# Hybrid conformer / RWKV-7 block: the A products of the RWKV chunks on 64 rows, and two scratch pools in PSUM resized

## The chip, the cores and the metric

The kernel runs on one core of a Trainium2 chip. The metric is the device time of one execution in microseconds (us), lower is better. The engines named below are TensorE (PE, with its weight loads shown apart as PEld), VectorE (DVE), ScalarE (ACT), GpSimd (POOL) and SyncE (SP), which issues the transfers.

## The reference, cut to what matters

One decoder block on x of 2048 tokens by 1024 channels, in fp32. A normalized and modulated input goes through one wide projection; its columns feed a convolution branch, an RWKV-7 branch and gates; both branches are projected, merged, projected once more and added to x. The part that the change touches is in the RWKV branch, a recurrence with a 64 x 64 state for each of 16 heads:

```python
def step(state, inp):
    r_t, w_t, k_t, v_t, kk_t, b_t = inp
    sk = jnp.einsum('bhvk,bhk->bhv', state, kk_t)
    state = (state * w_t[:, :, None, :] - sk[..., None] * b_t[:, :, None, :]
             + v_t[..., None] * k_t[:, :, None, :])
    return state, jnp.einsum('bhvk,bhk->bhv', state, r_t)
```

The kernel computes this recurrence in chunks of 64 tokens. Within a chunk every token's r and kk vector must meet every earlier token's k and b vector of the same head. These dot products over the head's 64 channels are what is called the A products here; a head's channels never meet another head's.

## The kernel before, in words

**Blocks, groups, pairs.** The sequence is cut into four blocks of 512 tokens (NB, TB), a block into eight chunks of 64 (NCH, CH). A tile of 128 partitions holds the channels of two heads, 64 rows each, which the code calls a pair; two pairs make a group, so a block has four groups (the loop from line 874, which calls `group`, line 575, which steps two `pair` generators, line 457, in the order ORD). The large projections go through `mm3k` (lines 198 to 206): each fp32 product is made of three products of fp32r halves, and its matmuls, all of line 205, fill TensorE's queue between everything else.

**One pair.** `pair` builds two tensors of 128 partitions, KR and BK, which hold, for each two chunks, 256 columns: those of the even chunk and those of the odd chunk, 128 each (kk and r side by side in KR, b and k in BK). KR is written on lines 498 and 523, BK on lines 512 and 518. Then come the A products (lines 528 to 541): for each half of the block (c4, four chunks) and each head (hh) four fp32 matmuls of 128 x 128 with BK's columns as weights and KR's columns streamed, into one PSUM bank pA; line 539 masks the bank on DVE and writes it to Asb. A tile's two heads lie in different row halves and a matmul contracts over all 128 rows. So line 531 first copies each head's 64 rows of BK, on ACT, into BKz, a tile whose other 64 rows were set to zero once (lines 287 to 289), and line 537 contracts BKz with all rows of KR. BKz has one buffer: the second half's copies wait for the first half's matmuls. The trace shows each of these fp32 matmuls as two records, so 512 of them are 1024 records. Later POOL scales BK in place (line 564) and PE transposes it (line 570).

**What follows.** `group` inverts the small triangular blocks (POOL, lines 625 to 630, and matmuls 659 and 668), and then runs the chain over the eight chunks (lines 677 to 702): matmuls 686, 691 and 697, each followed by a DVE instruction (688, 693, 701) that reads the chain's PSUM tile `xo`; line 701 writes the state S, which line 686 of the next chunk reads. Lines 599 and 710 are further products on 64-wide tiles: line 599 takes 64 rows of its operands and writes 64 partitions and goes from one half to the other with every matmul; line 710 contracts over all 128 rows and alternates the written half; line 691 stays in one half for all four matmuls of a chunk.

**PSUM.** Eight banks: two for the projections (pool pm, tag "main"), one for late products (pl), one for the convolution's accumulator (pc), PXB = 2 for the chain's `xo` (px) and PAB = 2 for scratch (pa, tag "aux"). Scratch serves, in this order within a pair, pw, pq, pss, pA four times, pv, pb and pt twice, and in a group pv of line 595. At the very start `hprep0` (line 379) fills four banks with the first projections (T_LORA and T_K in pm, T_R and T_V in px), and `shifted` (line 424) reads them later.

**What sets the order.** The program runs under a tile framework that finds the dependences, inserts the waits and writes the order of each engine's queue from a simulated timeline of its own; only the ORD and FILL tables and a few priorities are by hand. Every engine then works through its queue in that order.

Of the kernel before, what the change touches and what calls it, by code (L numbers as in the profile page):

```python
# [9 lines left out]
F32 = mybir.dt.float32  # L10
# [3 lines left out]
ALU = mybir.AluOpType  # L14
# [4 lines left out]
P = 128  # L19
D = 1024  # L20
KT = D // P
TB = 512
NTT = TB // P
CH = 64
NCH = TB // CH
# [10 lines left out]
HB = 8  # L36
HXB = 7
GG = 0
PXB, PAB = 2, 2
VVT, SHT, RKT, RHT, YT = "r", "sh", "k", "sh", "M"  # L40
ORD = (0, 0, 1, 0, 1, 1)
OE, LE, CE = 0, 0, 1
# [40 lines left out]
def hybrid_block(ctx: ExitStack, tc: tile.TileContext, x, vecs, convk, w2a2, final_g, ada, w_in, w_co, w_ro, w_o, crow, out,  # L83
                 seq=2048, groups=(0, 1, 2, 3), phase2=True, dbg=None):
    nc = tc.nc
# [36 lines left out]
    def rsqrt(y, x_, pool, eng, t=None):  # L122
        if t is None:
            t = pool.tile(list(x_.shape), F32, name="rs_t", tag="rs_t")
        eng.tensor_scalar(out=y.bitcast(I32), in0=x_.bitcast(I32), scalar1=-0.5, scalar2=float(0x5F3759DF),
                          op0=ALU.mult, op1=ALU.add)
        for _ in range(3):
            eng.tensor_tensor(out=t, in0=y, in1=y, op=ALU.mult)
            eng.scalar_tensor_tensor(out=t, in0=t, scalar=-0.5, in1=x_, op0=ALU.mult, op1=ALU.mult)
            eng.scalar_tensor_tensor(out=y, in0=t, scalar=1.5, in1=y, op0=ALU.add, op1=ALU.mult)  # L130

    def flat(ap):
        return ap.rearrange("p a b -> p (a b)")
# [41 lines left out]
    def load_w(name, n, hl=None):  # L175
        if hl is None:
            hl = [whl.tile([P, KT, P], F32R, name=n_, tag="w", bufs=WB) for n_ in ("w_hi", "w_lo")]
        hi, lo = hl
        back = kept.get((name, n))
        if back is not None:  # L180
            nc.sync.dma_start(hi.bitcast(F32), back[0].bitcast(F32))
            nc.sync.dma_start(lo.bitcast(F32), back[1].bitcast(F32))
            return hi, lo
        st = whl.tile([P, KT, P], F32, name="w_st", tag="w", bufs=WB)
        nc.sync.dma_start(st, wsrc[name][n])
        wcount[0] -= 1
        with tc.high_priority(HP):
            nc.scalar.copy(hi, st)  # L188
            lo_eng = nc.vector if wcount[0] >= 0 or (wcount[0] < -1000 and wcount[0] % 4 < W2) else nc.gpsimd
            lo_eng.tensor_tensor(out=lo, in0=st, in1=hi.bitcast(F32), op=ALU.subtract)  # L190
        if name in KEPT:
            i = "_".join(str(k) for k in (n if isinstance(n, tuple) else (n,)))
            kept[(name, n)] = [dp.tile([P, KT, P], F32R, name=f"k{p_}_{name}{i}", tag=f"k{p_}_{name}{i}") for p_ in "hl"]
            nc.sync.dma_start(kept[(name, n)][0].bitcast(F32), hi.bitcast(F32))
            nc.sync.dma_start(kept[(name, n)][1].bitcast(F32), lo.bitcast(F32))
        return hi, lo
# [50 lines left out]
    pm = ctx.enter_context(tc.tile_pool(name="pm", bufs=2, space=PSUM))  # L247
    c1 = late.enter_context(tc.tile_pool(name="c1", bufs=1))
# [3 lines left out]
    px = late.enter_context(tc.tile_pool(name="px", bufs=PXB, space=PSUM))  # L252
# [5 lines left out]
    pa = late.enter_context(tc.tile_pool(name="pa", bufs=PAB, space=PSUM))  # L258
# [23 lines left out]
    def headsum(ps, full, hi):  # L282
# [1 line left out]
        nc.gpsimd.tensor_tensor(out=lo, in0=full, in1=hi.bitcast(F32), op=ALU.subtract)  # L284
        nc.tensor.matmul(ps, bones, hi, start=True, stop=False)
        nc.tensor.matmul(ps, bones, lo, start=False, stop=True)
    BKz = c1.tile([P, 2, NCH // 4, 4 * CH], F32, name="BKz")
    nc.gpsimd.memset(BKz[64:128, 0], 0.0)
    nc.gpsimd.memset(BKz[0:64, 1], 0.0)
    hones = bones.bitcast(F32)[:, 0::64]  # L290
    keepm = c1.tile([P, TB // 2], mybir.dt.bfloat16, name="keepm")
    nc.vector.memset(keepm, 1.0)
# [1 line left out]
    maskA = c1.tile([P, 4, CH], F32, name="maskA")  # L294
# [36 lines left out]
    def hx(name):  # L331
        return xp.tile([P, TB], F32, name=name, tag="hx")
# [27 lines left out]
    def hsplit(h, k, src):  # L360
        hi = hp.tile([P, TB], F32R, name="h_hi", tag="h_hi", bufs=HB)
        lo = hp.tile([P, TB], F32R, name="h_lo", tag="h_lo", bufs=HB)
        with tc.high_priority(HP):
            nc.scalar.copy(hi, src)
            nc.vector.tensor_tensor(out=lo, in0=src, in1=hi.bitcast(F32), op=ALU.subtract)
        h[0].append(hi)
        h[1].append(lo)
# [9 lines left out]
    front = {}  # L377

    def hprep0(xs, ada_steps):


        ss = e2.tile([P, 5, NTT], F32, name="ss0", tag="ss0", bufs=1)
        s2, ss, rs, rt = ss[:, 0:2, :], ss[:, 2, :], ss[:, 3, :], ss[:, 4, :]
        for tt in range(NTT):
            for half in range(2):
                nc.scalar.activation(hx("xsq0"), xs[tt][:, half * TB:half * TB + TB], AF.Square,
                                     accum_out=s2[:, half, tt:tt + 1])
        nc.vector.tensor_tensor(out=ss, in0=s2[:, 0, :], in1=s2[:, 1, :], op=ALU.add)
        nc.vector.tensor_scalar(out=ss, in0=ss, scalar1=1.0 / D, scalar2=RMS_EPS, op0=ALU.mult, op1=ALU.add)
        rsqrt(rs, ss, None, nc.vector, rt)  # L390
        dg = e2.tile([P, NTT, P], F32, name="dg", tag="yj", bufs=1)
        for tt in range(NTT):
            nc.vector.tensor_scalar(out=dg[:, tt, :], in0=ident, scalar1=rs[:, tt:tt + 1], scalar2=None, op0=ALU.mult)
        h = ([], [])
        tiles_ = (T_LORA, T_K, T_R, T_V)
        wf_ = {}
        for k in range(KT):
            next(ada_steps)
            pt = (pl, pc)[k % 2].tile([P, NTT, P], F32, name="ps_x", tag=("late", "acc")[k % 2])
            for tt in range(NTT):  # L400
                nc.tensor.matmul(pt[:, tt, :], xs[tt][:, k * P:(k + 1) * P], dg[:, tt, :], start=(tt == 0),
                                 stop=(tt == NTT - 1), skip_group_check=True)
            hf = hx("hf0")
            nc.scalar.activation(hf, flat(pt), AF.Identity, scale=g_col[:, k:k + 1], bias=shift_col[:, k:k + 1])
            hsplit(h, k, hf)
            for i, ti in enumerate(tiles_):
                if k == i // 2:
                    hl = None
                    if i >= 2:
                        hl = [l3.tile([P, KT, P], F32R, name="w_f", tag="tk", bufs=TKB) for _ in range(4 - i)]  # L410
                        if i == 3:
                            hl.append(lt.tile([P, KT, P], F32R, name="w_f", tag="La", bufs=1))
                    wf_[ti] = load_w("in", ti, hl)
                    front[ti] = (pm, px)[i // 2].tile([P, TB], F32, name="ps_f", tag=("main", "xo")[i // 2])

            for i, ti in enumerate(tiles_):
                if ti in wf_ and k > i // 2:
                    for kk in range(0 if k == i // 2 + 1 else k - 1, k):
                        mm3k(front[ti], wf_[ti], h, kk)
        for ti in tiles_:  # L420
            mm3k(front[ti], wf_[ti], h, KT - 1)
        return h
# [34 lines left out]
    def pair(b, q_, pr, h, lora, uv, Asb, rn, res):  # L457
# [30 lines left out]
        KR = l3.tile([P, NCH // 2, 4 * CH], F32, name="KR", tag="KR", bufs=KRB)  # L488
        BK = l3.tile([P, NCH // 2, 4 * CH], F32, name="BK", tag="BK", bufs=BKB)
# [14 lines left out]
        for c in range(NCH):  # L504
            nc.tensor.matmul(pss[prow(c % 2), c // 2, :], sq[:, c * CH:c * CH + CH], hones, start=True, stop=True,
                             skip_group_check=True)
# [19 lines left out]
        yield  # L526

        for c4 in range(NCH // 4):
            for hh in range(2):
                hs = slice(64 * hh, 64 * hh + 64)  # L530
                nc.scalar.copy(BKz[hs, hh], BK[hs, c4 * 2:c4 * 2 + 2])  # L531
            for hh in range(2):
                pA = pa.tile([P, 2, 256], F32, name="aux", tag="aux")
                for c in range(4):
                    cc, e = (c4 * 4 + c) // 2, c % 2
                    es = slice(e * 128, e * 128 + 128)
                    nc.tensor.matmul(pA[:, c // 2, es], BKz[:, hh, c // 2, es], KR[:, cc, es],  # L537
                                     start=(c == 0), stop=(c == 3), skip_group_check=True)
                nc.vector.tensor_tensor(  # L539
                    out=Asb[:, hh, c4 * 4:c4 * 4 + 4, :].rearrange("p (a e) n -> p a (e n)", e=2),  # L540
                    in0=pA, in1=flat(maskA).unsqueeze(1).broadcast_to([P, 2, 256]), op=ALU.mult)
        for e in range(2):
            sl = prow(e)
            tri = Asb[sl, :, e::2, kcol(e)]
# [21 lines left out]
        for c4 in range(NCH // 4):  # L566
            pt = pa.tile([P, 4, P], F32, name="aux", tag="aux")
            for c in range(4):
                cc, e = (c4 * 4 + c) // 2, c % 2
# [5 lines left out]
    def group(b, g, h, lora, fill):  # L575
        uv = l3.tile([P, NCH, 2, P], F32, name="uv", tag="uv", bufs=2)
        As = [l3.tile([P, 2, NCH, P], F32, name="As", tag="As", bufs=ASB) for _ in range(2)]
        R = [{}, {}]
        rn = lt.tile([P, 2, NCH // 2, 2], F32, name="rn", tag="rn")
        pairs = [pair(b, q, 2 * g + q, h, lora, uv, As[q], rn, R[q]) for q in range(2)]  # L580
        for i, q in enumerate(ORD):
            next(pairs[q])
# [413 lines left out]
    pa = ctx.enter_context(tc.tile_pool(name="pa2", bufs=1, space=PSUM, reuse_waits="tile"))  # L996
# [162 lines left out]
```

## Time and profile before

| | us |
|---|---|
| three timed runs | 3060.63, 3069.59, 3058.7 |
| their median | 3060.63 |
| the profiled execution, time | 3065.4 |
| the profiled execution, span in the trace | 3063.7 |

The profiled execution took 1.7 us beside its span. The profile says how long each engine was busy, groups instructions by the kernel's line, says what ended an engine's idle time, and lists instructions in order of time. In the timeline view a row gives the start in us, the us from the first start to the last end, engine, line, operation, output<-inputs, the tile of the PE array (rows*columns), the streamed shape and the count of merged instructions. Matmuls overlap in the pipeline, so the distance from one start to the next, not the length of a record, says what a matmul costs TensorE.

### The profile page before, as it was taken

The page shows a single profiled execution, that of the slowest core. Times are in us where ns is not written, and L with a number is a line of the kernel's source. Part 1 is how long each engine was busy: PE and PEld are TensorE (multiplying, and loading weights), DVE is VectorE, ACT ScalarE, POOL GpSimd, SP SyncE. Part 2 cuts the span into 40 slices and gives each one's busy share as a digit, 9 for nine tenths or more (in the row PEclk, how much of TensorE's full clock was granted, in tenths as well). Part 3 has the DMA queues.
Part 4 walks back from the last instruction along what each step waited for, and adds up shares of the span by engine and source line. Part 5 has one row for each costly group of instructions (what it writes and reads, how often), then busy time and mean ns, then how long its engine had stood idle before and what let it go on. Part 6 is the DMA issues. An engine that isn't in the chain of part 4 may idle for free.

```text
span 3063.7 us, 64834 instructions
## 1 busy us (share of the span) xinstructions
PE 2884.4 (94%) x25672; PEld 2724.3 (89%) x25672; DVE 2056.4 (67%) x3879; ACT 1011.7 (33%) x1887; POOL 1257.8 (41%) x1788
## 2 busy tenths in 40 slices
PE   6789898999999999999999999999999999899998
PEld 5789897989999999999999999999989878678988
DVE  6677767786767676777677677767598445766333
ACT  4424343434233242424242424132433113333101
POOL 3455554533453435243434446426367016544000
PEclk9989999999999999999999999999999999999999
DMA  8766757674748477548576787546447678978674
GB/s 301 218 234 210 246 197 257 229 235 150 236 153 258 148 243 242 185 156 273 169 262 199 250 290 267 175 153 214 158 154 265 201 273 312 330 281 309 223 275 173
DMA packets 366368, 697.15 MB, mean 228 GB/s; under 512 B 135984, under 2 KB 154736, under 8 KB 366064
## 3 DMA queue, kind: packets, MB, share of 16 engines
q1 hardware_dynamic: 366064, 693.00, 67.2%
q8 instruction: 202, 3.31, 0.4%
q14 instruction: 102, 0.84, 0.1%
HBM read 504.04 MB, written 187.70 MB: 226 GB/s over the span
## 4 chain that ended last, share of the span: by engine, by line
PE 46%; DMA 17%; DVE 14%; POOL 11%; issue 5%; SPq 3%; ACT 3%; POOLq 0%; DVEq 0%; ACTq 0%
PE ps_main L205 31%; DMA w_st<-w_in_t 3%; DVE acc L776 3%; POOL TT L629 3%; POOL itmp L627 3%; PE aux L537 3%; DMA w_gr<-grow_d 2%; DMA La<-dA 2%; DMA w_st<-w_ro_t 2%; PE pout L1081 1%; PE pout L1079 1%; PE pout L1080 1%; PE xo L691 1%; DMA w_lo<-kl_in 1%; PE xo L697 1%
## 5 line engine op out<-in xcount | busy, mean ns | idle before, releaser
L205 PE MATMUL ps_main<-h_hi,w_hi 128*128 128x256 f32 x4608 | 958.6, 286 | 37.0 <-ACT w_hi L188 19.2
L205 PE MATMUL ps_main<-h_hi,w_lo 128*128 128x256 f32 x4608 | 960.9, 286 | 12.0 <-POOL w_lo L190 6.3
L205 PE MATMUL ps_main<-h_lo,w_hi 128*128 128x256 f32 x4608 | 961.1, 286 | 0.0
L205 PEld LDWEIGHTS ps_main<-h_hi,w_hi 128*128 128x128 f32 x4608 | 723.9, 191 | 47.3 <-ACT w_hi L188 26.1
L205 PEld LDWEIGHTS ps_main<-h_hi,w_lo 128*128 128x128 f32 x4608 | 722.2, 191 | 21.4 <-POOL w_lo L190 7.5
L205 PEld LDWEIGHTS ps_main<-h_lo,w_hi 128*128 128x128 f32 x4608 | 723.4, 191 | 5.4 <-issue 0.2
L776 DVE SCALAR_TENSOR_TENSOR acc<-u,ck,acc 128x512 f32<-128x512 f32 x928 | 698.3, 752 | 19.3
L627 POOL TENSOR_TENSOR itmp<-La,TT 128x126 f32<-128x126 f32 (+22 forms) x496 | 180.2, 363 | 138.5 <-DMA La<-dA 103.0
L629 POOL TENSOR_TENSOR TT<-TT,itmp 128x126 f32<-128x126 f32 (+22 forms) x496 | 189.1, 381 | 37.0
L190 POOL TENSOR_TENSOR w_lo<-w_st,w_hi 128x1024 fp32r<-128x1024 f32 x47 | 113.1, 2407 | 124.2 <-ACT w_hi L188 110.0
L683 ACT ACTIVATE Se<-S,pe 128x128 f32<-128x128 f32 x256 | 89.0, 395 | 195.8 <-DVE S L701 190.8
L537 PE MATMUL aux<-KR,BKz 128*128 128x128 f32 x1024 | 139.1, 285 | 12.3 <-ACT BKz L531 6.6
L701 DVE TENSOR_TENSOR S<-xo,Se 64x128 f32<-64x128 f32 x256 | 73.5, 287 | 112.3 <-PE xo L697 104.2
L537 PEld LDWEIGHTS aux<-KR,BKz 128*128 128x128 f32 x1024 | 127.7, 198 | 15.2 <-ACT BKz L531 8.5
L188 ACT CAST w_hi<-w_st 128x1024 fp32r<-128x1024 f32 x71 | 74.3, 1047 | 192.2 <-DMA w_st<-w_in_t 136.2
L693 DVE TENSOR_TENSOR uv<-xo,rn 64x256 f32<-64x256 f32 x128 | 53.8, 420 | 93.5 <-PE xo L691 92.1
L539 DVE TENSOR_TENSOR As<-aux,maskA 128x512 f32<-128x512 f32 x128 | 87.2, 688 | 40.8 <-PE aux L537 40.0
L688 DVE TENSOR_TENSOR XO<-xo,XO 128x256 f32<-128x256 f32 x128 | 53.7, 420 | 90.3 <-PE xo L686 76.2
L560 POOL TENSOR_TENSOR vv<-rk,vv 128x512 f32<-128x512 f32 x32 | 45.4, 1420 | 153.7 <-ACT rk L559 146.8
L788 ACT ACTIVATE th<-ps_main 128x512 f32<-128x512 f32 x64 | 38.1, 596 | 193.1 <-PE ps_main L205 186.5
L756 ACT ACTIVATE th<-ps_main 128x512 f32<-128x512 f32 x64 | 38.1, 596 | 180.1 <-PE ps_main L205 161.4
L531 ACT COPY BKz<-BK 64x512 f32<-64x512 f32 x128 | 79.0, 617 | 49.4 <-PE aux L537 32.1
(301 smaller groups left out, 5450.6 us busy)
## 6 DMA issues: line engine op xcount, KB each, us to landing
w_hi<-kh_in SPq DMA_DIRECT2D x219, 512.0 KB, 4.2
w_lo<-kl_in SPq DMA_DIRECT2D x219, 512.0 KB, 5.4
w_st<-w_in_t SPq DMA_DIRECT2D x73, 512.0 KB, 4.8
kh_in<-w_hi SPq DMA_DIRECT2D x71, 512.0 KB, 2.9
kl_in<-w_lo SPq DMA_DIRECT2D x71, 512.0 KB, 4.5
w_hi<-kh_ro SPq DMA_DIRECT2D x32, 512.0 KB, 5.0
w_lo<-kl_ro SPq DMA_DIRECT2D x32, 512.0 KB, 6.0
w_hi<-kh_co SPq DMA_DIRECT2D x32, 512.0 KB, 3.7
```

The source lines that it names most:

```text
L188: nc.scalar.copy(hi, st)
L190: lo_eng.tensor_tensor(out=lo, in0=st, in1=hi.bitcast(F32), op=ALU.subtract)
L205: nc.tensor.matmul(ps[:, qs], ww[:, k, :], aa[k][:, qs], start=(k == 0 and t == 0 and q == 0), stop=(k == KT - 1 and t == 2 and q == ms - ...
L531: nc.scalar.copy(BKz[hs, hh], BK[hs, c4 * 2:c4 * 2 + 2])
L537: nc.tensor.matmul(pA[:, c // 2, es], BKz[:, hh, c // 2, es], KR[:, cc, es], start=(c == 0), stop=(c == 3), skip_group_check=True)
L539: nc.vector.tensor_tensor(out=Asb[:, hh, c4 * 4:c4 * 4 + 4, :].rearrange("p (a e) n -> p a (e n)", e=2), in0=pA, in1=flat(maskA).unsqueeze ...
L627: nc.gpsimd.tensor_tensor(out=tmp[:, :ni, :nt], in0=La[:, j:j + 1, j + 1:].broadcast_to([P, ni, nt]), in1=TT[:, :ni, j:j + 1].broadcast_to ...
L629: nc.gpsimd.tensor_tensor(out=TT[:, :ni, j + 1:], in0=TT[:, :ni, j + 1:], in1=tmp[:, :ni, :nt], op=ALU.add)
L683: nc.scalar.mul(Se[:, q, :], Sg[:, q, :], R[q]["pe"][:, c:c + 1])
L693: nc.vector.tensor_tensor(out=uv[pr_, c].rearrange("p q (h n) -> p q h n", n=64), in0=xo[pr_, 0:2].rearrange("p q (h n) -> p q h n", n=64) ...
L701: nc.vector.tensor_tensor(out=Sg[hs, :, hs], in0=xo[hs, 2:4, hs], in1=Se[hs, :, hs], op=ALU.add)
L776: nc.vector.scalar_tensor_tensor(out=acc if i + 1 < HALO else yj, in0=u[:, i:i + TB], scalar=ck[:, j, i:i + 1], in1=acc, op0=ALU.mult, op1 ...
```

## The change

Three things. The A products of a head contract over the head's own 64 rows of BK and KR, without BKz; the copies, the tile and its two memsets go. The two heads' matmuls alternate, head 0 into one bank, head 1 into another, so the two banks of one c4 are taken together and masked after all eight matmuls are issued. The scratch pool has three banks in place of two, the chain's pool one in place of two, and of the four first projections T_V moves to a scratch bank.

```diff
-PXB, PAB = 2, 2
+PXB, PAB = 1, 3
...
-    BKz = c1.tile([P, 2, NCH // 4, 4 * CH], F32, name="BKz")
-    nc.gpsimd.memset(BKz[64:128, 0], 0.0)
-    nc.gpsimd.memset(BKz[0:64, 1], 0.0)
...
-                    front[ti] = (pm, px)[i // 2].tile([P, TB], F32, name="ps_f", tag=("main", "xo")[i // 2])
+                    fp_, ft_ = ((pm, "main"), (pm, "main"), (px, "xo"), (pa, "aux"))[i]
+                    front[ti] = fp_.tile([P, TB], F32, name="ps_f", tag=ft_)
...
         for c4 in range(NCH // 4):
+            pA = [pa.tile([P, 2, 256], F32, name="aux", tag="aux") for _ in range(2)]
+            for c in range(4):
+                cc, e = (c4 * 4 + c) // 2, c % 2
+                es = slice(e * 128, e * 128 + 128)
+                for hh in range(2):
+                    hs = slice(64 * hh, 64 * hh + 64)
+                    nc.tensor.matmul(pA[hh][:, c // 2, es], BK[hs, cc, es], KR[hs, cc, es],
+                                     start=(c == 0), stop=(c == 3), skip_group_check=True)
             for hh in range(2):
-                hs = slice(64 * hh, 64 * hh + 64)
-                nc.scalar.copy(BKz[hs, hh], BK[hs, c4 * 2:c4 * 2 + 2])
-            for hh in range(2):
-                pA = pa.tile([P, 2, 256], F32, name="aux", tag="aux")
-                for c in range(4):
-                    cc, e = (c4 * 4 + c) // 2, c % 2
-                    es = slice(e * 128, e * 128 + 128)
-                    nc.tensor.matmul(pA[:, c // 2, es], BKz[:, hh, c // 2, es], KR[:, cc, es],
-                                     start=(c == 0), stop=(c == 3), skip_group_check=True)
                 nc.vector.tensor_tensor(
                     out=Asb[:, hh, c4 * 4:c4 * 4 + 4, :].rearrange("p (a e) n -> p a (e n)", e=2),
-                    in0=pA, in1=flat(maskA).unsqueeze(1).broadcast_to([P, 2, 256]), op=ALU.mult)
+                    in0=pA[hh], in1=flat(maskA).unsqueeze(1).broadcast_to([P, 2, 256]), op=ALU.mult)
```

## Prediction

> **What bounds the kernel now.** I read the page's busy times first, then the same by stage, then what TensorE waited for.
>
> ```profile
> span 3063.7 us, 64834 instructions
> ...
> PE 2884.4 (94%) x25672; PEld 2724.3 (89%) x25672; DVE 2056.4 (67%) x3879; ACT 1011.7 (33%) x1887; POOL 1257.8 (41%) x1788
> ```
>
> ```profile
> 93.00:700.00 607.00, 555.10 (x5274) 534.85 (x5275) 446.38 (x770) 234.57 (x392) 297.89 (x401) 0.95 0.68 227
> 700.00:1300.00 600.00, 582.17 (x5734) 564.29 (x5733) 421.17 (x817) 206.93 (x398) 247.07 (x413) 0.99 0.63 202
> 1300.00:1900.00 600.00, 583.23 (x5759) 564.29 (x5758) 425.40 (x797) 212.36 (x406) 265.75 (x424) 0.99 0.71 232
> 1900.00:2310.00 410.00, 396.30 (x3901) 382.74 (x3901) 295.26 (x547) 132.62 (x239) 195.89 (x312) 0.97 0.54 174
> ```
>
> The second fence is the view of stretches: length, then busy us of PE, PEld, DVE, ACT and POOL, the granted clock and the share of the DMA engines. These four stretches hold all A products. PE is busy for 2116.8 of 2217 us, idle for 4.5%; DVE, the next, is busy for 1588.2 (72%), ACT for 786.5 (35%). So TensorE sets the time, and microseconds taken from its queue should shorten the end; work taken from ACT should not, except where PE waited for it. "Busy" alone doesn't say how much a matmul costs, since records overlap; for that I use distances between starts.
>
> ```profile
> L537 PE MATMUL aux<-KR,BKz 128*128 128x128 f32 x1024 | 139.1, 285 | 12.3 <-ACT BKz L531 6.6 <-DVE As L539 4.3 <-DVE ss L128 1.2
> L539 DVE TENSOR_TENSOR As<-aux,maskA 128x512 f32<-128x512 f32 x128 | 87.2, 688 | 40.8 <-PE aux L537 40.0
> L531 ACT COPY BKz<-BK 64x512 f32<-64x512 f32 x128 | 79.0, 617 | 49.4 <-PE aux L537 32.1 <-POOL BK L518 13.6 <-DVE r L436 2.4
> ```
>
> These are the three groups that the change touches. The A products are 1024 records, and PE stood idle ahead of them for only 12.3 us in all: what is to be won lies in the records, not in the waits.
>
> **What an A-product record costs now.** One stretch of PE's timeline gives it, with its neighbours:
>
> ```profile
> 262.01 0.40 PE L205 MATMUL ps_main<-h_lo,w_hi 128*128 128x256 f32 x2
> 262.24 1.95 PE L537 MATMUL aux<-KR,BKz 128*128 128x128 f32 x16
> 263.94 0.48 PE L205 MATMUL ps_main<-h_hi,w_lo 128*128 128x256 f32 x2
> 264.26 0.40 PE L205 MATMUL ps_main<-h_hi,w_hi 128*128 128x256 f32 x2
> 264.59 0.68 PE L691 MATMUL xo<-XO,As 64*64 64x64 f32 x8
> 265.20 0.51 PE L205 MATMUL ps_main<-h_lo,w_hi 128*128 128x256 f32 x2
> 265.54 0.40 PE L205 MATMUL ps_main<-h_hi,w_lo 128*128 128x256 f32 x2
> 265.78 0.40 PE L205 MATMUL ps_main<-h_hi,w_hi 128*128 128x256 f32 x2
> ```
>
> Two projection records take 265.78 - 265.54 = 0.24, or 118 ns each. From 262.01 to 264.26 are 2.25 us with 2 + 16 + 2 records; less four at 118 ns that leaves 1.78 us for 16 A-product records, 111 ns each. All 1024 cost 113.7 us of PE's queue.
>
> **What they cost afterwards: overlap.** Half the rows alone makes nothing shorter, since the streamed shape and the 128 weight columns stay. The gain can only come from two matmuls running at once in the two row halves. The trace has such pairs:
>
> ```profile
> 2374.75 0.28 PE L205 MATMUL ps_main<-h_hi,w_hi 128*128 128x256 f32 x1
> 2374.96 2.08 PE L599 MATMUL aux<-uv,As 64*64 64x64 f32 x64
> 2376.97 0.39 PE L205 MATMUL ps_main<-h_hi,w_hi 128*128 128x256 f32 x1
> 2377.19 0.40 PE L205 MATMUL ps_main<-h_lo,w_hi 128*128 128x256 f32 x2
> ...
> L599 PE MATMUL aux<-uv,As x1024: 218/218/313, 131.9 to 2376.8; 64*64 64x64 f32 x171
> L691 PE MATMUL xo<-XO,As x1024: 218/218/366, 208.5 to 2503.3; 64*64 64x64 f32 x171
> ```
>
> Lines 599 and 691 have the same shape and the same median record (218 ns). Line 599 changes its half with every matmul: 64 records lie between 2374.96 and 2376.97, at most (2.08 - 0.218) / 63 = 30 ns from start to start. Line 691 stays in one half: 8 records in 0.68 us, (0.68 - 0.218) / 7 = 66 ns, the first of them slowed by the entry. That is a ratio of about one half: pairs in different tiles do run at once, in fp32 too. But line 599's tiles differ in rows and in written partitions, while the new pair differs in rows alone: both heads write all 128 partitions, of two banks. A pair that differs in the other way alone is there too:
>
> ```profile
> 296.84 0.40 PE L205 MATMUL ps_main<-h_hi,w_hi 128*128 128x256 f32 x2
> 297.17 1.15 PE L710 MATMUL late<-uv,As 128*64 128x64 f32 x32
> 298.25 0.51 PE L205 MATMUL ps_main<-h_lo,w_hi 128*128 128x256 f32 x2
> ```
>
> Line 710 uses all rows and alternates the written half: 32 records in 1.15 us, about (1.15 - 0.22) / 31 = 30 ns, as quick as line 599. So columns alone suffice; rows alone no row here shows. The bounds for a record are thus 111 ns (no overlap) and 55.5 ns (full overlap); there is no row that would put it lower, as the 128 weight columns remain. I take 55.5, because line 599, with half the rows per matmul, is the nearest row and reaches the full factor: 1024 x 55.5 = 56.8 us.
>
> The Trainium skill, in "TensorE: Matmul & The Clock Gate" (Part 3, Packing small matmuls), says that weight loads overlap running matmuls only where the row groups differ, and reports 3.07 times for four row tiles of 32 rows. Line 710 contradicts its "only" (30 ns with all rows in use); for rows alone no run here shows it, and by that rule the streaming term would be the same 56.8 us.
>
> **What they cost afterwards: changes of tile shape.** Until now A products had the shape of the projections around them, 128*128. They become 64*128, and a change of shape is paid for. In the first timeline the eight records of line 691 take 1.28 us from 264.26 to 265.54 with four of line 205, so 0.81 us; for line 599, 2.44 us from 2374.75 to 2377.19 with two of them, so 2.20 us for 64. Taking the two equations s + 64 x 30 = 2200 and s + 8 x 60 = 810 (60 being twice line 599's distance), s is 280 and 330 ns; I use 330 ns for a burst, entry and exit together.
>
> The Trainium skill's rule in "TensorEngine Tiling (Array Packing)" (Key Properties) speaks against the change: a change of tiling mode drains the engine. The trace agrees, with these 330 ns.
>
> How many bursts? Along PE's timeline the A products now stand in 101 unbroken bursts; the first, one of the middle sort and the last:
>
> ```profile
> 93.03 6.42 PE L537 MATMUL aux<-KR,BKz 128*128 128x128 f32 x32 [5.64 <-ACT BKz L531]
> ...
> 266.13 1.05 PE L537 MATMUL aux<-KR,BKz 128*128 128x128 f32 x8
> ...
> 2306.27 1.05 PE L537 MATMUL aux<-KR,BKz 128*128 128x128 f32 x8
> ```
>
> If each half block were one burst, there would be 64. 101 bursts cost 33 us, 64 cost 21. I take 27: some bursts lie against line 691, whose neighbours change shape already, and without copies there is less reason to break them. So PE's queue loses 113.7 - 56.8 - 27 = 30 us.
>
> **The copies.** 128 copies of 617 ns leave ACT, 79.0 us. ACT is busy for 35% of the stage, so that is worth only what PE waited for it: 6.6 us, 5.64 of them in the one wait at 93.03. There two copies of 0.62 us lie between POOL's last write of BK and the first matmul, the rest is the wait for BK itself. I count 1.5 us. The two memsets are on POOL ahead of the first products, under work; nothing.
>
> **The banks.** The chain's second bank goes.
>
> ```profile
> PE xo L686 <- DVE S L701: 5.3, 6, 1.6
> PE aux L537 <- DVE As L539: 4.3, 3, 1.7
> POOL BK L564 <- ACT BKz L531: 22.5, 11, 5.1
> ```
>
> The next chunk's first matmul (line 686) reads the state that line 701 writes, and line 701 is also the last reader of the old bank. The wait for the data is therefore already the wait for the bank: no cost, and no gain from having had two. With the third scratch bank, one half block takes two and the next finds one free; its second matmul then waits for line 539's mask of the first bank. Before, it was the copies (0.62 us each, released by PE) that separated the two halves, for some 2.2 us (263.94 to 266.13), and the queue filled the gap with lines 205 and 691. PE lost 4.3 us to masks and 6.6 to copies over 64 halves, so I expect it filled again: 0. If the cover is gone, see below. At the very start T_V's bank is one of the three scratch banks; two are left there, as before.
>
> On POOL line 564 waited for the copies (22.5 us in all); now it waits for the last A product of the pair, and behind it in POOL's queue stand the inversions of line 627 and weight splits. The last matmul ends about as much later (16 x 55.5 = 0.9 us) as two copies of 0.62 us fall away: no difference counted.
>
> **The sum.** 30 + 1.5 = 31.5 us off PE's queue. PE is idle 4.5% of this stage, which I double for waits that hid behind the longer queue: a tenth goes back, 28 us are left. Against the profiled execution, 3065.4 - 28 = 3037; that one lies 4.8 us above the median of 3060.63, and against the median the forecast is 3033 us.
>
> **The rivals.**
>
> No overlap: two row halves that write the same partitions run one after the other, 111 ns a record, and the changes of shape come on top: +27 - 1.5 = +25.5, so 3086 us, slower. For it speaks that no row shows rows alone, and that both heads need each PSUM partition; against it, that they use two banks and that line 599's row halves do overlap. It decides above (113.7 - 27) / 1024 = 85 ns a record. The same price would follow if the order written out put all of one head first. 0.15.
>
> The gain turns into a wait: the second half's bank isn't masked when PE comes to it, and nothing is put between. A mask takes 0.69 us, and with the end of the matmul ahead of it about 1 us for each of 32 pairs: 32 us against 31.5 won, so 3061 us, no change. Against it stand the 4.3 us of today, for it that both masks now start only behind eight matmuls. A queue that breaks the bursts up further (two more for each pair, 64 x 0.33 = 21 us) comes to nearly the same, 3052. 0.22.
>
> More than forecast: 64 bursts, and of the 12.3 us of idle time ahead of the A products most goes: 56.9 - 21 + 10 = 46, so 3015. 0.05. The forecast itself, with bursts from 64 to 101 and up to a fifth given back: 0.58.
>
> **How the numbers follow.** The forecast's own range is 3023 (64 bursts, nothing given back: 37 us) to 3040 (101 bursts, a fifth given back: 20 us). No overlap (0.15) stays outside above; the range goes down to 3014 for the larger gain and up to 3069, past the eaten gain. A measurement of this kernel can tell about 0.5%, 15 us, from no change. Faster by more: 0.58 + 0.05, less a little for the edge, 0.61; within: 0.22; slower: 0.17, of which 0.02 for an order that turns out worse elsewhere.
>
> **What would show it.** In the changed profile the A products stand as 64*128 with starts alternately a few ns and some 105 ns apart, mean near 55, and PE's time from the burst's start to the next projection is about 1.2 us for 16 records in place of 1.78. Bursts number between 64 and 101, and ACT's busy time is down by 79 us. PE's wait for line 539 stays under 10 us in total; line 686's wait for line 701 stays near 5. The no-overlap rival shows starts 111 ns apart throughout; the bank rival shows waits of PE for line 539 near 30 us. The forecast is wrong if PE's idle time in the four stretches, 100 us now, grows by more than 10.

## The result and the profile after

Five runs of the changed kernel have a median of 3042.17 us (3037.27 to 3049.32), five of the kernel before, on the same chip, 3064.1 us (3058.7 to 3069.59). The ratio is 0.9945 with a 95% interval of 0.9924 to 0.9965, so about 17 us less (11 to 23); the bare medians lie 22 us apart. A second set of nine runs, on another occasion, gave 0.9956 (0.9939 to 0.9973). The forecast was 28 us less. Faster it is; but the experiments below show that it is not faster for the reason given.

First the page's head, then the stretches of the changed kernel (columns as before: length, busy us of PE, PEld, DVE, ACT, POOL, clock, DMA share, GB/s):

```profile
span 3047.6 us, 64674 instructions
...
PE 2879.3 (94%) x25672; PEld 2698.9 (89%) x25672; DVE 2062.4 (68%) x3879; ACT 935.7 (31%) x1759; POOL 1255.3 (41%) x1786
```

```profile
93.00:700.00 607.00, 552.67 (x5278) 527.29 (x5277) 450.26 (x780) 220.50 (x369) 299.10 (x403) 0.95 0.69 227
700.00:1300.00 600.00, 575.00 (x5653) 552.83 (x5652) 417.30 (x793) 178.19 (x348) 238.81 (x406) 0.98 0.62 200
1300.00:1900.00 600.00, 586.75 (x5743) 562.20 (x5742) 428.20 (x800) 193.27 (x372) 259.38 (x420) 0.99 0.69 228
1900.00:2310.00 410.00, 404.03 (x4029) 385.54 (x4029) 303.97 (x558) 121.19 (x222) 208.68 (x319) 0.98 0.57 182
```

ACT is relieved of 76 us, nearly the 79 of the copies, and nothing follows from that. PE's busy time fell by 5.1 us only (2884.4 to 2879.3), though half of the A products should have vanished under the other half. What else fell is PE's idle time: 3063.7 - 2884.4 = 179.3 us before, 3047.6 - 2879.3 = 168.3 after. A second profiled execution of the changed kernel has PE busy for 2872.3 us and idle for 164.0, so 5 us of busy time is within what two executions of one kernel differ by.

Now the changed groups on the page:

```profile
L533 PE MATMUL aux<-KR,BK 64*128 64x128 f32 x1024 | 112.7, 292 | 5.4 <-POOL KR L521 3.3
L561 POOL TENSOR_TENSOR BK<-BK,pe 128x1024 f32<-128x1024 f32 x32 | 61.2, 1912 | 119.4 <-PE aux L533 102.5
L536 DVE TENSOR_TENSOR As<-aux,maskA 128x512 f32<-128x512 f32 x128 | 83.4, 684 | 34.0 <-PE aux L533 33.2
```

And from the view of PE's waits (us in total, times, longest), with, as the second line, what line 533 waited for of the masks (us, times):

```profile
PE xo L683 <- DVE S L698: 5.2, 4, 3.0
  DVE As L536: 0.3, 1
```

(Line numbers moved: 533 was 537, 536 was 539, 561 was 564, 683 was 686.) The chain's single bank costs nothing: the wait for the state is 5.2 us, as it was 5.3. For the masks PE waited 0.3 us in all. The shape is 64*128, as it should be. The queue shows what went wrong:

```profile
261.97 0.28 PE L205 MATMUL ps_main<-h_hi,w_lo 128*128 128x256 f32 x1
262.18 1.60 PE L533 MATMUL aux<-KR,BK 64*128 64x128 f32 x20
263.71 0.67 PE L688 MATMUL xo<-XO,As 64*64 64x64 f32 x8
264.31 0.71 PE L533 MATMUL aux<-KR,BK 64*128 64x128 f32 x4
264.95 0.39 PE L205 MATMUL ps_main<-h_hi,w_lo 128*128 128x256 f32 x1
265.18 0.40 PE L205 MATMUL ps_main<-h_hi,w_hi 128*128 128x256 f32 x2
...
266.12 0.40 PE L205 MATMUL ps_main<-h_lo,w_hi 128*128 128x256 f32 x2
266.45 1.16 PE L533 MATMUL aux<-KR,BK 64*128 64x128 f32 x8
267.53 0.50 PE L205 MATMUL ps_main<-h_hi,w_lo 128*128 128x256 f32 x2
267.88 0.38 PE L694 MATMUL xo<-uv,tk 128*128 128x128 f32 x2
```

Within the 20 records the distances from start to start are, in ns, 7, 206, 7, 105, 7, 105 and so on for the first sixteen, then 112, 111, 112. So the overlap is real, 56 ns a record. But it holds for the first half block alone. There the two heads alternate. In the second half block head 0's four matmuls (8 records) follow at once, in the third scratch bank, at 112 ns each; head 1's four come 2 us later as a burst of their own, 8 records at 112 ns, because their bank has to be masked first. That is the picture in nearly all of the 32 pairs: 31 bursts have exactly 8 records, and the first record of each of them waits for the semaphore that the masks on DVE update. Of the distances between A-product records 254 are under 30 ns, where pairing throughout would give 512. There are 82 bursts.

### The profile page after: what moved, and what is told of

It is laid out like the page before. It is cut to its first block, busy times and chain, and to the rows that moved or that the text cites. A ratio compares the mean times of both kernels' runs of the same rounds, so it can differ in the third digit from the quotient of the medians.

```text
span 3047.6 us, 64674 instructions
## 1 busy us (share of the span) xinstructions
PE 2879.3 (94%) x25672; PEld 2698.9 (89%) x25672; DVE 2062.4 (68%) x3879; ACT 935.7 (31%) x1759; POOL 1255.3 (41%) x1786
## 4 chain that ended last, share of the span: by engine, by line
PE 51%; DMA 18%; DVE 11%; POOL 10%; SPq 4%; issue 4%; ACT 2%; POOLq 0%; DVEq 0%; ACTq 0%
PE ps_main L205 36%; POOL TT L626 3%; POOL itmp L624 3%; DVE acc L773 3%; PE aux L533 2%; DMA w_st<-w_ro_t 2%; DMA w_st<-w_in_t 2%; DMA La<-dA 2%; PE xo L688 2%; DMA w_st<-w_co_t 1%; PE pout L1077 1%; PE pout L1078 1%; PE pout L1076 1%; PE xo L683 1%; PE xo L694 1%
## 5 line engine op out<-in xcount | busy, mean ns | idle before, releaser
L205 PEld LDWEIGHTS ps_main<-h_hi,w_hi 128*128 128x128 f32 x4608 | 725.6, 191 | 54.1 <-ACT w_hi L188 29.7
L533 PE MATMUL aux<-KR,BK 64*128 64x128 f32 x1024 | 112.7, 292 | 5.4 <-POOL KR L521 3.3
L533 PEld LDWEIGHTS aux<-KR,BK 64*128 64x128 f32 x1024 | 96.0, 194 | 16.3 <-POOL KR L521 3.8
L561 POOL TENSOR_TENSOR BK<-BK,pe 128x1024 f32<-128x1024 f32 x32 | 61.2, 1912 | 119.4 <-PE aux L533 102.5
L430 ACT ACTIVATE t<-ps_main,mu 128x512 f32<-128x512 f32 x96 | 65.8, 686 | 124.6 <-PE ps_main L205 105.7
L785 ACT ACTIVATE th<-ps_main 128x512 f32<-128x512 f32 x64 | 38.2, 596 | 191.8 <-PE ps_main L205 181.7
L688 PE MATMUL xo<-XO,As 64*64 64x64 f32 x1024 | 90.1, 226 | 3.8 <-DVE XO L685 2.1
```

The lines of the kernel that those rows point to most:

```text
L205: nc.tensor.matmul(ps[:, qs], ww[:, k, :], aa[k][:, qs], start=(k == 0 and t == 0 and q == 0), stop=(k == KT - 1 and t == 2 and q == ms - ...
L430: nc.scalar.activation(t1, ps, AF.Identity, scale=mu1[:, mi:mi + 1])
L533: nc.tensor.matmul(pA[hh][:, c // 2, es], BK[hs, cc, es], KR[hs, cc, es], start=(c == 0), stop=(c == 3), skip_group_check=True)
L688: nc.tensor.matmul(xo[pr_, q, hs], As[q][pr_, hh, c, kcol(e)], XO[pr_, c, q, hs], start=(q == 0 and hh == 0), stop=(q == 1 and hh == 1), s ...
```

## The experiments

Five theories, named as in the expectations. **R**, as forecast: the overlap of the row halves brought the gain. **Q**: the queue is worth what the traces price it at, overlap (0.112 us for each overlapped pair of records) less changes of shape (0.33 to 0.39 us a burst), and that comes out even here. **B**: the banks brought it. **P**: the path of a pair without the copies brought it. **O**: the scheduler wrote another order, with less idle time for PE, and the rows have no part in it. Ratios are to the kernel before on the same chip, in the same set of runs.

**Banks alone.** The kernel before with the new bank counts and T_V's place.

```diff
-PXB, PAB = 2, 2
+PXB, PAB = 1, 3
```

> The kernel before with the new bank counts (one for the chain, three for scratch, T_V's first projection in scratch), and nothing else. Theory Q (the end follows TensorE's queue alone): the A products cost the queue what they cost before, so no change, ratio 1.000 within 0.003. Theory B (the banks brought the gain): the third scratch bank shortens waits, ratio about 0.995, as for the whole change. Theory P (the path of a pair without the ACT copies brought it): no change here.

Measured 1.0022 (1.0009 to 1.0035). B falls: banks alone bring nothing, they cost 7 us.

**No copies.** The kernel before without line 531.

```diff
-                nc.scalar.copy(BKz[hs, hh], BK[hs, c4 * 2:c4 * 2 + 2])
...
-                    nc.tensor.matmul(pA[:, c // 2, es], BKz[:, hh, c // 2, es], KR[:, cc, es],
+                    nc.tensor.matmul(pA[:, c // 2, es], BK[:, cc, es], KR[:, cc, es],
```

> The kernel before with its old banks, without the ACT copies: the matmuls of both heads read all 128 rows of BK and KR, so each product also sums the other head's rows, which the reference does not do; the work on TensorE has the same size and shape. Theory P: 79 us less on ACT and a shorter path of a pair bring most of the gain, ratio 0.995 to 0.996. Theories Q and B: only PE's 7 us of waits for copies at most, ratio 0.998 to 1.000.

Measured 1.0012 (1.0001 to 1.0023). P falls. 79 us off ACT are worth nothing to the end, as the prediction had it.

**The change again, and the change on all rows.** The second kernel differs from the first in the operands of one statement. The scheduler wrote the same order for both, on all five engines, so no difference of order can mix in.

```diff
-                    nc.tensor.matmul(pA[hh][:, c // 2, es], BK[hs, cc, es], KR[hs, cc, es],
+                    nc.tensor.matmul(pA[hh][:, c // 2, es], BK[:, cc, es], KR[:, cc, es],
```

> The changed kernel once more, beside the next three on one chip. Its earlier ratio is 0.9945 from five runs; expected 0.993 to 0.998 by any theory. It is the base for the next kernel.

> The changed kernel with its A-product matmuls on all 128 rows of BK and KR in place of the head's 64 (each product then also sums the other head's rows, which the reference does not do). The order built is the same on every engine, instruction for instruction; only the form of 512 matmuls differs: no overlap and no change of shape. Theory R (the overlap of the halves brought the gain, as forecast): the gain goes, ratio 1.000 or more. Theory Q (queue price by the traces): 254 overlapped records save 28 us and 82 bursts cost 27 to 32 us, so it is even: same as the changed kernel within 4 us, ratio 0.994 to 0.996; then the gain came with the other order (theory O).

Measured 0.9956 (0.9939 to 0.9973) and 0.9940 (0.9919 to 0.9962). Without row halves, without any overlap, the gain is all there. R falls, in the plainest way. The two ratios differ by 0.0016, give or take 0.003, so by the end the row halves are worth nothing that can be told from zero. (The mean granted clock of the two sets of runs differs as well, 0.975 and 0.978.) The same place of the queue as above, in the kernel on all rows:

```profile
257.64 0.28 PE L205 MATMUL ps_main<-h_hi,w_lo 128*128 128x256 f32 x1
257.76 2.40 PE L533 MATMUL aux<-KR,BK 128*128 128x128 f32 x20
260.08 0.68 PE L688 MATMUL xo<-XO,As 64*64 64x64 f32 x8
260.69 0.71 PE L533 MATMUL aux<-KR,BK 128*128 128x128 f32 x4
261.16 0.36 PE L205 MATMUL ps_main<-h_hi,w_lo 128*128 128x256 f32 x1
261.36 0.40 PE L205 MATMUL ps_main<-h_hi,w_hi 128*128 128x256 f32 x2
...
262.30 0.40 PE L205 MATMUL ps_main<-h_lo,w_hi 128*128 128x256 f32 x2
262.54 1.05 PE L533 MATMUL aux<-KR,BK 128*128 128x128 f32 x8
263.35 0.48 PE L205 MATMUL ps_main<-h_hi,w_lo 128*128 128x256 f32 x2
263.67 0.60 PE L694 MATMUL xo<-uv,tk 128*128 128x128 f32 x4
```

From the first row to the row after the second gap of shapes it takes 261.36 - 257.64 = 3.72 us, in the changed kernel 265.18 - 261.97 = 3.21: 0.51 won. From the x2 row ahead of the lone burst to line 694 it takes 263.67 - 262.30 = 1.37 us, in the changed kernel 267.88 - 266.12 = 1.76: 0.39 lost, since eight records in a shape of their own cost two changes and overlap nothing. That leaves 0.12 us a pair at this place, so an estimate of 4 us over 32 pairs, in PE's queue. Whole traces can be compared too, since the order is the same: added up over all distances from start to start that touch an A-product record, and the two behind each of them (leaving out those over 0.6 us in any of the traces), the changed kernel is 1.1 us shorter than the kernel on all rows, and 3.0 us in its second profiled execution. That is Q.

**One half for both.** Same order, same shape, but the heads share a row half, so that nothing can overlap.

```diff
-                    hs = slice(64 * hh, 64 * hh + 64)
+                    hs = slice(0, 64)
```

> The changed kernel, but both heads' A products read rows 0 to 63 of BK and KR (head 1's products are then head 0's). Same order on every engine, same shape of 64 rows, same banks; the two heads now lie in one row half, so nothing can overlap, and the changes of shape stay. Theory Q: 254 records no longer overlapped, 254 x 0.112 = 28 us over the changed kernel, ratio to before about 1.004; against the same order on all rows (0.994) that is the price of the changes alone, 82 x 0.33 to 0.39 less the edges beside other shapes, 24 to 30 us. If it lies within 5 us of the changed kernel, overlap is worth nothing to the end.

Measured 1.0024 (1.0010 to 1.0037). The same place once more:

```profile
268.01 0.28 PE L205 MATMUL ps_main<-h_hi,w_lo 128*128 128x256 f32 x1
268.23 2.50 PE L533 MATMUL aux<-KR,BK 64*128 64x128 f32 x20
270.65 0.68 PE L688 MATMUL xo<-XO,As 64*64 64x64 f32 x8
271.26 0.71 PE L533 MATMUL aux<-KR,BK 64*128 64x128 f32 x4
271.89 0.39 PE L205 MATMUL ps_main<-h_hi,w_lo 128*128 128x256 f32 x1
272.12 0.40 PE L205 MATMUL ps_main<-h_hi,w_hi 128*128 128x256 f32 x2
...
273.06 0.40 PE L205 MATMUL ps_main<-h_lo,w_hi 128*128 128x256 f32 x2
273.39 1.16 PE L533 MATMUL aux<-KR,BK 64*128 64x128 f32 x8
274.48 0.50 PE L205 MATMUL ps_main<-h_hi,w_lo 128*128 128x256 f32 x2
274.82 0.60 PE L694 MATMUL xo<-uv,tk 128*128 128x128 f32 x4
```

Here it takes 4.11 and 1.76 us, together 0.78 more than on all rows and 0.90 more than with overlap. Over 32 pairs that is an estimate of 25 us for the changes of shape and of 29 us that the overlap returns; the sums over the whole traces are 26.7 us for the changes and 27.8 to 29.7 for the overlap. The end says the same with less resolution: 1.0024 - 0.9940 is 26 us for the changes; 1.0024 less 0.9945 or 0.9956 is 21 to 24 us for the overlap, each give or take some 8.

**Heads apart, and its twin on all rows.** The changed kernel with the two loops exchanged; and the kernel before without copies, with the new banks, whose order on every engine is the same.

```diff
+            for hh in range(2):
+                hs = slice(64 * hh, 64 * hh + 64)
+                for c in range(4):
+                    cc, e = (c4 * 4 + c) // 2, c % 2
+                    es = slice(e * 128, e * 128 + 128)
+                    nc.tensor.matmul(pA[hh][:, c // 2, es], BK[hs, cc, es], KR[hs, cc, es],
```

> The changed kernel with the loops of head and chunk exchanged: all four products of head 0, then all four of head 1, so almost no neighbours of different heads (62 in the order built, of them one for most bursts, in place of 250; 88 bursts in place of 82). It shows what overlap was worth. Theory Q: 190 x 0.112 + 6 x 0.39 = 24 us more than the changed kernel, about 3066 us, ratio to before 1.001. Theories B and P: as the changed kernel, ratio 0.995.

> The kernel before with the new banks and without copies, its A products on all 128 rows (they also sum the other head's rows). Its order on every engine is that of the run with the heads apart, instruction for instruction, so the pair differs only in the form of the A products: there 168 overlapped records and 88 bursts of another shape. Theory Q: the form there costs 88 x 0.39 - 168 x 0.112 = 15 us less some edges beside bursts that change shape anyway, so this one is 10 to 15 us faster than that one, ratio to before 1.000 to 1.002. Theory R: overlap counts more than the changes, so this one is slower than that one, ratio above 1.005. Theory P or B with both together (copies gone and a third bank): 0.995.

Measured 1.0052 (1.0035 to 1.0069) and 1.0008 (0.9993 to 1.0023). In this order the 64-row form costs 13 us by the end and 13.3 us by the sum of distances as above, as Q has it (10 to 15), where R has the other sign. The twin also shows that banks and missing copies together, with the heads one after the other, bring nothing.

**Heads paired in both halves.** First a chain of issue order that makes the heads alternate throughout; then the same with these matmuls preferred by the scheduler (issued within `tc.high_priority(HP)`); then that on one row half (`hs = slice(0, 64)`), in the same order as the second. The lines below are those of the first.

```diff
-                for hh in range(2):
+                for hh in (1, 0):
                     hs = slice(64 * hh, 64 * hh + 64)
-                    nc.tensor.matmul(pA[hh][:, c // 2, es], BK[hs, cc, es], KR[hs, cc, es],
-                                     start=(c == 0), stop=(c == 3), skip_group_check=True)
+                    with (tc.issue_after(mA) if mA is not None else ExitStack()):
+                        mA = nc.tensor.matmul(pA[hh][:, c // 2, es], BK[hs, cc, es], KR[hs, cc, es],
+                                              start=(c == 0), stop=(c == 3), skip_group_check=True)
+                    mA = mA.ins if hasattr(mA, "ins") else mA
```

> The changed kernel with head 1 first and every A-product matmul queued behind the one before it, so that in both halves of a block the heads alternate. In the order built, 424 neighbours are of different heads where the changed kernel has 250, in 88 bursts in place of 82. Theory Q: each further pair saves 0.112 us and each further burst costs 0.39 us of the queue, 174 x 0.112 - 6 x 0.39 = 17 us less than the changed kernel, about 3025 us, ratio to before 0.989. Theories B and P: the queue of A products isn't what moved, so ratio 0.995 as for the change.

> The kernel with the heads paired in both halves, and its A-product matmuls given the scheduler's high priority, so that the chain's matmuls break them less: 74 bursts in place of 88 and 82, 438 neighbours of different heads in place of 424 and 250. Theory Q: against the changed kernel 188 x 0.112 + 8 x 0.39 = 24 us less of the queue; from its own order, a few us either way. Against before: 1024 records at 0.112 less 438 x 0.112, plus 74 x 0.39: 20 us less, ratio 0.993, or 0.988 if the changed kernel's order is kept. Theory R with no price for changes of shape: 49 us less, 0.984. Theory O alone: anything between 0.995 and 1.002.

> The kernel with the heads paired in both halves and its A products first, with both heads reading rows 0 to 63 (head 1's products are then head 0's). Same order as that kernel on every engine, same shape, no overlap. Theory Q: some 440 overlapped records gone, 49 us over that kernel (ratio 1.0025), so 1.018. If that kernel's overlap was lost to waits that end no sooner, the difference is far smaller, 1.003 to 1.010.

Measured 0.9961 (0.9949 to 0.9974), 1.0025 (1.0008 to 1.0043) and 1.0117 (1.0094 to 1.0141). The first has 446 overlapped records in the trace (424 were expected), and yet isn't faster than the change (expected 0.989); the second should have been at 0.993 and is slower than before. So Q, too, does not forecast the end where the order differs. Within one order it does better: without overlap the second kernel loses 28 us (give or take 9), of 49 expected. The pages say where the rest is:

```profile
span 3064.4 us, 64742 instructions
...
PE 2880.5 (94%) x25672; PEld 2697.7 (88%) x25672; DVE 2068.6 (68%) x3879; ACT 932.0 (30%) x1759; POOL 1257.5 (41%) x1786
```

```profile
span 3102.5 us, 64742 instructions
...
PE 2934.4 (95%) x25672; PEld 2754.4 (89%) x25672; DVE 2066.8 (67%) x3879; ACT 932.9 (30%) x1759; POOL 1256.2 (40%) x1786
```

With overlap (first fence) PE is busy for 53.9 us less and idle for 183.9 us; without it, 168.1. Of the queue's gain 16 us come back as idle time.

**The old form in the new emission.** Zero-padded copies and all 128 rows, as before, but both banks taken together, heads by turns, and the new bank counts; then the same with the old counts.

```diff
+            for hh in range(2):
+                hs = slice(64 * hh, 64 * hh + 64)
+                nc.scalar.copy(BKz[hs, hh], BK[hs, c4 * 2:c4 * 2 + 2])
             pA = [pa.tile([P, 2, 256], F32, name="aux", tag="aux") for _ in range(2)]
...
-                    nc.tensor.matmul(pA[hh][:, c // 2, es], BK[hs, cc, es], KR[hs, cc, es],
+                    nc.tensor.matmul(pA[hh][:, c // 2, es], BKz[:, hh, c // 2, es], KR[:, cc, es],
```

> The zero-padded copies and all-row matmuls of before, with the changed kernel's emission: two banks taken together, heads by turns, one bank for the chain and three for scratch. No tile shape changes, no overlap. Theory O, in the form that this emission and these banks make the better order: 0.994 to 0.996. Theory O, in the form that any new order may fall either way: between 0.995 and 1.003, and nothing follows from where it falls. Theory R: 1.000.

> The previous run's kernel (zero-padded copies, all rows, two banks taken together, heads by turns), with the banks of before: two for the chain, two for scratch, T_V's first projection in the chain's pool. The previous run took 0.991 of before with one and three. Banks alone, with the heads one after the other, gave 1.002. If the emission by turns is the cause alone: 0.991 to 0.994 here too. If it needs the third scratch bank (with two, each half block holds all the scratch there is until its masks are done): 1.000 or more.

Measured 0.9912 (0.9894 to 0.9931) and 1.0080 (1.0066 to 1.0094). The first has the lowest ratio of all, 27 us under the kernel before; it is faster than the change, but not clear of the change on all rows (0.9940, 0.9919 to 0.9962). Neither row halves nor missing copies are in it. Its page, then the other's:

```profile
span 3030.3 us, 64930 instructions
...
PE 2876.0 (95%) x25672; PEld 2714.2 (90%) x25672; DVE 2048.3 (68%) x3879; ACT 1015.1 (33%) x1887; POOL 1263.6 (42%) x1788
```

```profile
span 3081.1 us, 64881 instructions
...
PE 2888.4 (94%) x25672; PEld 2729.7 (89%) x25672; DVE 2056.3 (67%) x3879; ACT 1012.3 (33%) x1887; POOL 1253.8 (41%) x1788
```

Both do the work of the kernel before, with as many instructions on each engine, and differ from it in order and, the first, in banks. PE is idle for 154.3 us in the first and 192.7 in the second, against 179.3 before; the mean granted clock is 0.979, 0.968 and 0.975. So 51 us lie between two orders of the same work: 38.4 us of idle time and 12.4 us of busy time. The clock bears on the second. In the traces it stands at 0.5 for 3.4 to 20.5 us at a time, some 130 us in all in the first kernel and some 200 in the second, and these stretches come behind idle time: in the second, the 7 us ahead of one hold 2.4 us of it in the median, where any 7 us hold 0.4 on average. In the kernel before, for one, PE waits 2.34 us up to 1875.83 us, and from 1876.85 to 1878.98 the records of line 205 start 213 ns apart in place of 118. So an idle gap can cost more than its own length, and an order that leaves more gaps can pay for them in busy time too. It isn't one wait that moves, and none of the longest of the slower one is at the A products (line 205 are projections, 742 a group's transposes, 401 the start, 687 the chain):

```profile
PE ps_main L205 <- ACT w_hi L188: 21.7, 4, 11.7
PE late L742 <- POOL XO L737: 20.0, 3, 17.1
PE ps_x L401 <- DVE dg L393: 19.0, 1, 19.0
PE xo L687 <- DVE S L702: 16.8, 8, 3.9
```

Heads by turns with two scratch banks is the worst of the four combinations, with three the best; heads one after the other with two and with three lie at 1.000 and 1.0022. That fits the idea that a half block which takes two banks at once needs a third for everything else. But each of the four is one order that the scheduler happened to write, and other orders on one and the same set of banks lie 0.6 to 0.7% apart (0.9940 and 1.0008, 0.9961 and 1.0025 above), against 1.7% here. So the idea is argued, not shown, and why one order leaves PE idle for less is left open.

## Why the prediction was right in its range and wrong in its reason

The time fell as forecast, and 3042 us lies in the stated range of 3014 to 3069, though above the forecast's own 3023 to 3040. That it came so close is luck: the term that was to bring 30 us brought 1 to 4, and the gain came with an order that could as well have cost something. Most of the signs named ahead appeared (82 bursts, ACT down by 76 us, 0.3 us for the masks, starts 7 and 105 ns apart where the heads alternate). The one that could have told, a mean distance near 55 ns, did not appear over all bursts, and it was not put as a count of overlapped records.

- **What bounds the kernel**: right. PE's queue stays nearly full (98.6 us idle in the four stretches, 100.2 before), and ACT's 76 us were worth nothing.
- **Cost of a record now, 111 ns**: right; the twin on all rows shows the same distances.
- **Overlap, 55.5 ns**: right where the heads alternate (7 and 105 ns). The bound that no row had shown, rows alone, is settled: row halves that write the same partitions of two banks do run at once. The no-overlap rival falls.
- **"1024 x 55.5 = 56.8 us"**: this is the step that failed. 254 pairs of records overlapped, not 512, so the term is 113.7 - 254 x 0.112 = 85.3 us. The cause stands in the prediction itself, under the banks: "one half block takes two and the next finds one free; its second matmul then waits". I asked only whether PE would wait there, and priced it at 0; an order with one head first is named only in a sentence of the no-overlap rival. PE didn't wait (0.3 us for masks); the scheduler gave it head 0's other three matmuls in place of waiting, and so took the pairs apart. The queue paid for the missing bank in its order and not in time.
- **Changes of shape, 27 us**: right; 25 to 27 us by the queue and 26 by the end. One burst costs 0.39 us where it stands alone between projections (1.76 us less four records of line 205 at 118 ns and eight at 112), not 0.33, and 82 bursts were in the range given. The Trainium skill's rule ("TensorEngine Tiling (Array Packing)", Key Properties) that a change of tiling mode drains the engine agrees with these 0.39 us a burst, though no run here shows that a drain is what they consist of. At this size of burst the changes eat nearly the whole overlap.
- **30 us off the queue**: so it was 1 to 4 us by the traces, and not distinguishable from nothing by the end (0.9945 and 0.9956 against 0.9940).
- **A tenth given back**: too little in one case, open in the other. Where one order was kept, 28 of 49 us (give or take 9) and 21 to 24 of 29 (give or take some 8) reached the end.
- **What the prediction didn't have**: that the new program gets another order from the scheduler, and that this alone moves the end. Six orders of the same all-row matmuls gave 0.9912, 0.9940, 1.0008, 1.0012, 1.0022 and 1.0080. The 17 us of the change lie within that spread and stay without row halves; so the gain belongs to the order that the new program got, with its banks, and why this order is a good one is open. A term of +-0.8% for the order belonged beside the sum.
- **POOL's line 564**: "no difference counted" was wrong in itself, its wait went from 62 us (for copies and masks) to 102.5 (for the last A products, which in the second half come late); nothing shows that the end felt it.

## What to carry to other kernels

Packing two 64-row matmuls into one array pays only if the burst is long and unbroken: here a pair of records saves 0.112 us and each burst of another shape costs 0.39, so that a burst breaks even at seven records (0.39 / 0.056), all of them paired. Count the buffers for the pair, not for the matmul: a spare bank for one of two partners lets a scheduler run it ahead alone. And where a scheduler writes the order, compare forms at one and the same order (change operands, not structure, until the order is identical) before crediting the form; otherwise the order's own scatter, here 0.991 to 1.008, is what one measures.

## What the runs showed of the hardware that was not expected

With the heads apart, head 1's matmuls did not wait for all of head 0's. In a burst of 16 records at 1594.87 us (the trace's own records, not merged) the first start about 112 ns apart, then some come in pairs 4 to 6 ns apart until head 0's last, which updates its semaphore, and then the rest at 112 ns:

```
starts of the 16 matmul records, us
1594.869 1595.082 .194 .305 .417 .423 .529 .636 .640 .748 .752 .860 .971 1596.083 .195 .306
(.423 waits for a semaphore; .752 updates the one that says that a bank is complete)
```

Head 0's eight are those at 869, 082, 194, 305, 417, 529, 640 and 752, 112 ns apart after the first; head 1's first one, at 423, stands behind all of them in the queue and starts with head 0's fifth. That the queue has them so is seen in the twin on all rows, whose order is the same: there the record that updates the semaphore is the eighth of the 16 and the one that waits the ninth, where here they start as the eleventh and the sixth. So a record for a free row half overtook three others here. That is why even this kernel had 168 overlapped records, with 62 neighbours of different heads in its queue, and why it isn't quite so, as said at the start, that every engine works through its queue in order. The Trainium skill's statement in "TensorE: Matmul & The Clock Gate" (Part 3, Packing small matmuls) that matmuls keep strict order in start and end does not hold for the starts in this trace.
